# A hybrid SSD and retention block on one core: small products of several pieces placed at one step

## The chip, the cores and the metric

The kernel runs on one core of a Trainium2 chip. The metric is device time in microseconds (us), the median of the runs. The core has a matrix engine (TensorE, "PE" in the profile), VectorE ("DVE"), ScalarE ("ACT"), GpSimd ("POOL") and SyncE ("SP"), whose queue issues nearly all transfers here. Products are written to PSUM banks, and VectorE or ScalarE must read a bank before the next product may be written to it.

## What is computed

One decoder block over 1024 tokens of width 1024, in float32:

```python
h = rmsnorm(x, norm1_w)
z, xbc, dt, q, k, v, g = split(h @ w_in)          # width 5648
y_ssd = ssd_mixer(z, xbc, dt, ...)   # conv + SiLU, chunks of 128, 16 heads of 64, 2 groups
y_ret = retention_mixer(q, k, v, g)  # rotary q/k, chunks of 128, 8 heads of 128
x = x + concat(y_ssd, y_ret) @ w_out
h = rmsnorm(x, norm2_w)
x = x + (silu(h @ w_gate) * (h @ w_up)) @ w_down
out = rmsnorm(x, final_norm_w)
```

Within a chunk both mixers form scores, weight them with a decay matrix, multiply them with the values, add the product of the running state, and bring the state forward. These are products of 64 to 128 columns beside the wide projections.

## The kernel before, in words

The tokens are worked in two halves of 512 (four chunks of 128). Everything on TensorE is one list of *steps*: a step is one slice of 128 rows of a weight block times four tiles, each as three products of 512 columns (`three`), so 12 products. Steps 0 to 95 are the twelve input blocks of half 0, steps 96 to 191 those of half 1 (eight steps each), 192 to 223 the output projection of half 0, 224 to 255 that of half 1; the feed-forward part follows. `run_all` walks the list: for each step it loads and divides the weights of some later steps (`advance`), emits the 12 products, and then whatever was hung on that step with `at(step, function)`. A block's results are taken out of PSUM by `evac` at its last step, with high priority.

The mixers are such hung functions, laid over a stretch of steps by `spread`, which maps a list of (place, function) linearly onto it, the last place onto the last step:

- `ssd_pieces` (one round for each chunk and group, eight a half): `s0` loads the row of decays (E); `sz` loads the gate z; `s1` has a transpose and the B-C scores into one bank `bc` and four transposes of x into a bank `xp` and much VectorE and ScalarE work that makes the decay matrix E; `s2` has 16 products into a bank `yp` and one of 512 columns into a bank `sp`. VectorE then reads `yp` four times (line 685), multiplies by the gate (line 688), and adds `sp` to the state S (lines 700 and 701). `s3` has two one-column sums. A small float32 product appears as two instructions (two passes), a transpose as one. Half 0 lies on steps 64 to 93, half 1 on steps 152 to 185.
- `ret_pieces` (one round a chunk): `r1` loads v and g and has 8 score products; `r2` has 24 products (scores times values, the old state, the new state) and makes the normalised result `yn` on VectorE in a chain of some 40 instructions that ends at line 807; `r3` transposes `yn` in two lots of four (banks emptied by ScalarE at line 819) and stores it. Half 0 lies on steps 98 to 142, half 1 on steps 198 to 221.
- The q/k blocks rotate each of four token tiles (`rope`) and transpose them (`turn(t)`), one bank for each turn.

All small products take their banks from one tag, `M`, of three buffers; the input and output blocks use a tag `L` of five. Products keep their order in the program. The order of the instructions on VectorE and ScalarE is made when the program is built, from readiness and from priority (program order, moved forward for weight division and `evac`); on the chip each engine then runs its queue in that fixed order.

Of the kernel before, what the change touches and what calls it, by code (L numbers as in the profile page):

```python
# [65 lines left out]
def block_kernel(ctx: ExitStack, tc: tile.TileContext, x, norm1_w, w_in, conv_w, conv_b,  # L66
# [161 lines left out]
    def at(i, f):  # L228
        hooks.setdefault(i, []).append(f)
# [243 lines left out]
    def qk_block(h, b):  # L473

        d = H[h]
        c0, n = ((C_DT, 272), (C_Q + 256, 384), (C_K + 128, 384))[b]
        q0, nq, k0, nk = ((0, 4, 0, 0), (4, 4, 0, 2), (0, 0, 2, 6))[b]
        nh = nq + nk
        np_, p0 = nh // 2, (0, 2, 5)[b]

        def v(a):
            return a.rearrange("p (h j d) -> p h j d", j=2, d=32)

        def begin(blk):
            if b == 0:
                d["qk"] = T([P, 8, TH], "qk")
                d["ktok"] = T([P, NT, RH * RD], "ktok")
                d["dtr"] = T([P, NT, SH], "dtr", bufs=2)
            ev, rr = {}, {}

            def rope(t):
                def f():
                    g = h * NT + t
                    ab = T([P, 2, 512], f"m{14 + t % 2}")
                    A, B = ab[:, 0, :nh * RD], ab[:, 1, :nh * RD]
                    r = rr[t] = ev[t // 2][:, t % 2, :]

                    def bc(k):
                        return kc[:, k + 32 * g:k + 32 * g + 32].unsqueeze(1).unsqueeze(1) \
                            .to_broadcast([P, nh, 2, 32])  # L500
                    en = v(r[:, :nh * RD])
                    tt(v(A), en, bc(K_COS), op=ALU.mult)
                    tt(v(B), en, bc(K_SIN), op=ALU.mult)
                    ro = v(r[:, :nh * RD])
                    tt(ro[:, :, 0, :], v(A)[:, :, 0, :], v(B)[:, :, 1, :], op=ALU.subtract)
                    tt(ro[:, :, 1, :], v(B)[:, :, 0, :], v(A)[:, :, 1, :], op=ALU.add)
                    if nk:
                        nc.gpsimd.tensor_tensor(
                            d["ktok"][:, t, k0 * RD:(k0 + nk) * RD].rearrange(
                                "p (h d) -> p h d", d=RD),  # L510
                            r[:, nq * RD:nh * RD].rearrange("p (h d) -> p h d", d=RD),
                            kc[:, K_KD + k0:K_KD + k0 + nk].unsqueeze(2).to_broadcast([P, nk, RD]),
                            op=ALU.mult)
                return f

            def turn(t):
                def f():
                    m = bank("M")
                    for j in range(np_):
                        tr(m[:, j * P:(j + 1) * P], rr[t][:, j * P:(j + 1) * P])  # L520
                    act(d["qk"][:, p0:p0 + np_, t * P:(t + 1) * P],
                        m[:, :np_ * P].rearrange("p (j q) -> p j q", q=P), AF.Copy)
                return f

            def evac(t, pss):
                ps = pss[t]
                o = 16 if b == 0 else 0
                if b == 0:
                    stt(d["dtr"][:, t, :], ps[:, :SH], d["rt"](t), dtb, op0=ALU.mult, op1=ALU.add)
                if t % 2 == 0:  # L530
                    ev[t // 2] = T([P, 2, 512], f"x{6 + t // 2}")
                e = ev[t // 2][:, t % 2, :]
                if nq:
                    stt(e[:, :nq * RD].rearrange("p (h d) -> p h d", d=RD),
                        ps[:, o:o + nq * RD].rearrange("p (h d) -> p h d", d=RD), d["rt"](t),
                        kc[:, K_QD + q0:K_QD + q0 + nq].unsqueeze(2).to_broadcast([P, nq, RD]),
                        op0=ALU.mult, op1=ALU.mult)
                if nk:
                    act(e[:, nq * RD:nh * RD], ps[:, o + nq * RD:o + nh * RD], AF.Copy,
                        scale=d["rt"](t))  # L540
                at(blk.last + (1, 2, 4, 5)[t], rope(t))
                at(blk.last + (4, 5, 7, 7)[t], turn(t))
            return evac
        return Block(False, lambda: d["hT"], [(w_in, c0, n)], begin)

# [60 lines left out]
    def ssd_pieces(h, W):  # L606
# [3 lines left out]
        def s0(c, g):  # L610
            def f():
                r0 = c * SH + g * 8
                E = st["E", c, g] = W([P, 8, P])
                nc.sync.dma_start(E, rD[h][r0:r0 + 8, :].partition_broadcast(P))
            return f

        def sz(c, g):
            def f():

                if g == 0:  # L620
                    st[c] = T([P, 8, P], f"x{4 + c % 2}")
                nc.sync.dma_start(
                    st[c][:, 4 * g:4 * g + 4, :],
                    zD[h][g][:, :, c * P:(c + 1) * P].rearrange("j p q -> p j q"))
            return f

        def s1(c, g):
            def f():
                ex, xbc = d["ex"], d["xbc"]
                cs = slice(c * P, (c + 1) * P)  # L630
                r0 = c * SH + g * 8
                first = h == 0 and c == 0
                E = st.pop(("E", c, g))
                bT, cT = xbc[4][:, g, cs], xbc[5][:, g, cs]
                bc = bank("M")
                tr(bc[:, :P], bT)
                mm(bc[:, P:2 * P], bT, cT)
                b2 = T([P, 2, P], "bc", bufs=2)
                btok, cbm = b2[:, 0, :], b2[:, 1, :]
                act(btok, bc[:, :P], AF.Copy)  # L640
                tt(cbm, bc[:, P:2 * P], tri, op=ALU.mult)
                xp = bank("M")
                for j in range(4):
                    ch = 4 * g + j
                    tr(xp[:, j * P:(j + 1) * P], xbc[ch // 2][:, ch % 2, cs])
                xw = W([P, 2, 512])
                xdte, xdt = xw[:, 0, :], xw[:, 1, :]
                tt(v8(xdt), v8(xp), hbc(d["dt"], c, g), op=ALU.mult)
                for q in range(8):
                    hs = slice(q * SP_, (q + 1) * SP_)  # L650
                    act(xdte[:, hs], xp[:, hs], AF.Copy, scale=d["dte"][:, r0 + q:r0 + q + 1])  # L651
                C = None
                if not first:
                    C = W([P, 8, P])
                    act(C, E, AF.Exp)
                    tt(C, C, cT.unsqueeze(1).to_broadcast([P, 8, P]), op=ALU.mult)
                for q in range(8):
                    ts(E[:, q, :], E[:, q, :], ex[:, 0, r0 + q:r0 + q + 1], 0.0,
                       op0=ALU.subtract, op1=ALU.min)
                act(E, E, AF.Exp)  # L660
                tt(E, E, cbm.unsqueeze(1).to_broadcast([P, 8, P]), op=ALU.mult)
                st[c, g] = E, C, btok, xdte, xdt
            return f
# [43 lines left out]
        def s3(c):  # L707
            def f():

                if c == 0:  # L710
                    d["ss"] = T([P, SG, NT], "ss", bufs=2)
                b = bank("M")
                for g in range(SG):
                    mm(b[:, g:g + 1], st.pop(("q2", c, g)), ones[:, :1])
                act(d["ss"][:, :, c], b[:, :SG], AF.Copy)
            return f
# [4 lines left out]
        o = []  # L721
        for i, (c, g) in enumerate(seq):
            p = 0.5 * i
            o += [(p - 0.2, s0(c, g)), (p, s1(c, g)), (p + 0.25, sz(c, g)), (p + 0.8, s2(c, g))]
            if g == 1:
                o.append((p + 1.2, s3(c)))
        return sorted(o, key=lambda q: q[0])


    def ret_pieces(h, W):  # L730
# [80 lines left out]
        def r3(c):  # L811
            def f():
                yn = st.pop(c)
                o = W([P, 8, P])
                for b in range(2):
                    m = bank("M")
                    for j in range(4):
                        tr(m[:, j * P:(j + 1) * P], yn[:, 4 * b + j, :])
                    act(o[:, 4 * b:4 * b + 4, :], m.rearrange("p (j q) -> p j q", q=P), AF.Copy)
                nc.sync.dma_start(mixD[h][1][:, :, c * P:(c + 1) * P].rearrange("j p q -> p j q"),  # L820
                                  o)
            return f
        o = []
        for c in range(NT):
            o += [(c, r1(c)), (c + 0.5, r2(c)), (c + 1.6, r3(c))]
        return sorted(o, key=lambda q: q[0])


# [599 lines left out]
    s0 = I0["z0"].first  # L1428
# [30 lines left out]
    s0 = GU  # L1459
# [38 lines left out]
```

## Time and profile before

| | |
|---|---|
| median of 3 runs | 1456.47 us (1455.24 to 1456.62) |
| profiled execution | 1455.97 us, span 1454.2 us |
| TensorE products | 1437.1 us busy, 7278 instructions |
| VectorE | 1091.5 us busy |
| ScalarE | 670.7 us busy |
| granted TensorE clock | 0.998 mean |
| idle TensorE that the waits view lists | 5.5 us in 9 waits |

A row of a timeline is: start in us, duration, engine, line, operation, output<-inputs, and how many instructions were merged; a bracket at its end is the idle time before it and what ended it. Since products are pipelined, the time of a run of products is read from the start of its row to the start of the next row.

### The profile page before, as it was taken

The page shows a single profiled execution, that of the slowest core. Times are in us where ns is not written, and L with a number is a line of the kernel's source. Part 1 is how long each engine was busy: PE and PEld are TensorE (multiplying, and loading weights), DVE is VectorE, ACT ScalarE, POOL GpSimd, SP SyncE. Part 2 cuts the span into 40 slices and gives each one's busy share as a digit, 9 for nine tenths or more (in the row PEclk, how much of TensorE's full clock was granted, in tenths as well). Part 3 has the DMA queues.
Part 4 walks back from the last instruction along what each step waited for, and adds up shares of the span by engine and source line. Part 5 has one row for each costly group of instructions (what it writes and reads, how often), then busy time and mean ns, then how long its engine had stood idle before and what let it go on. Part 6 is the DMA issues. An engine that isn't in the chain of part 4 may idle for free.

```text
span 1454.2 us, 20840 instructions
## 1 busy us (share of the span) xinstructions
PE 1437.1 (99%) x7278; PEld 1195.5 (82%) x7278; DVE 1091.5 (75%) x2263; ACT 670.7 (46%) x1296; POOL 35.8 (2%) x66
## 2 busy tenths in 40 slices
PE   9999999999999999999999999999999999999996
PEld 7889878888889888888888878888888888888885
DVE  5677788767688898468764889987777778566767
ACT  6334467444354656324454643544444445422223
POOL 1002000000000000000000000000000000000000
PEclk9999999999999999999999999999999999999999
DMA  7333466474425458736543345644434446997863
GB/s 248 111 97 105 136 195 192 124 238 117 138 66 164 151 160 263 250 124 205 181 143 112 99 145 169 245 180 145 149 134 141 156 145 264 356 386 236 294 183 133
DMA packets 142313, 257.41 MB, mean 177 GB/s; under 512 B 11332, under 2 KB 71040, under 8 KB 142208
## 3 DMA queue, kind: packets, MB, share of 16 engines
q1 hardware_dynamic: 141072, 254.40, 53.5%
q8 instruction: 57, 0.93, 0.3%
q10 hardware_dynamic: 736, 1.12, 0.2%
q0 software_dynamic: 400, 0.57, 0.1%
q14 instruction: 48, 0.39, 0.1%
HBM read 185.46 MB, written 70.58 MB: 176 GB/s over the span
## 4 chain that ended last, share of the span: by engine, by line
PE 94%; DVE 3%; DMA 1%; ACT 1%; issue 0%; SPq 0%; DVEq 0%; ACTq 0%
PE L L179 70%; PE M L179 22%; PE M L182 2%; DMA zD<-x 0%; DMA m<-rD 0%; DVE x L1246 0%; DMA wr<-in_w_in_dram 0%; DVE x L1268 0%; DMA kc<-in_consts_dram 0%; DVE x L448 0%; ACT m L651 0%; DVE x L452 0%; DVE x L1282 0%; DVE wp L268 0%; DVE x L1292 0%
## 5 line engine op out<-in xcount | busy, mean ns | idle before, releaser
L268 DVE TENSOR_TENSOR wp<-wr,wp 128x512 fp32r<-128x512 f32 (+2 forms) x248 | 162.4, 655 | 140.6 <-ACT wp L267 135.4
L267 ACT ACTIVATE wp<-wr 128x512 fp32r<-128x512 f32 (+2 forms) x248 | 150.0, 605 | 253.9 <-PE L L179 206.6
L179 PE MATMUL L<-h,wp 128*128 128x512 f32 x1128 | 266.2, 392 | 0.0
L179 PE MATMUL L<-wp,h 128*128 128x512 f32 (+2 forms) x1248 | 259.9, 364 | 0.3 <-DVE x L448 0.3
L179 PEld LDWEIGHTS L<-h,wp 128*128 128x128 f32 x1128 | 209.9, 188 | 44.6 <-issue 1.0
L179 PEld LDWEIGHTS L<-wp,h 128*128 128x128 f32 x1248 | 215.2, 188 | 31.0 <-issue 5.3
L179 PE MATMUL L<-wp,m 128*128 128x512 f32 x768 | 180.2, 392 | 0.0
L179 PEld LDWEIGHTS L<-wp,m 128*128 128x128 f32 x768 | 142.7, 188 | 30.3 <-issue 0.5
L179 PE MATMUL L<-m,wp 128*128 128x512 f32 x360 | 86.5, 389 | 0.0
L179 PE MATMUL L<-m,h 128*128 128x512 f32 x321 | 79.8, 393 | 1.5 <-ACT h L1391 1.4
L179 PEld LDWEIGHTS L<-m,wp 128*128 128x128 f32 x360 | 67.6, 188 | 14.0
L179 PEld LDWEIGHTS L<-m,h 128*128 128x128 f32 x321 | 59.8, 188 | 15.8 <-ACT h L1391 2.6
L179 PE MATMUL L<-m,x 128*128 128x512 f32 x288 | 69.2, 389 | 0.0
L179 PEld LDWEIGHTS L<-m,x 128*128 128x128 f32 x288 | 54.1, 188 | 11.2
L179 PE MATMUL M<-m,x 128*128 128x512 f32 x240 | 57.7, 389 | 0.0
L411 DVE SCALAR_TENSOR_TENSOR m<-m,cols,m 128x512 f32<-128x512 f32 x72 | 52.2, 747 | 3.5 <-ACT m L409 3.2
L179 PEld LDWEIGHTS M<-m,x 128*128 128x128 f32 x240 | 45.1, 188 | 9.4
L179 PE MATMUL L<-h,m 128*128 128x512 f32 x207 | 51.3, 389 | 0.0
L179 PE MATMUL M<-m,m 128*64 128x128 f32 (+2 forms) x354 | 48.4, 299 | 0.0
L179 PEld LDWEIGHTS L<-h,m 128*128 128x128 f32 x207 | 38.9, 188 | 8.1
L179 PE MATMUL L<-h,x 128*128 128x512 f32 x180 | 43.5, 390 | 0.0
L179 PE MATMUL M<-m,wp 128*128 128x512 f32 x168 | 41.0, 391 | 0.0
(321 smaller groups left out, 2329.4 us busy)
## 6 DMA issues: line engine op xcount, KB each, us to landing
wr<-in_w_in_dram SPq DMA_DIRECT2D x144, 256.0 KB, 2.7
aD<-ktok SPq DMA_DIRECT2D x49, 512.0 KB, 3.2
m<-aD SPq DMA_DIRECT2D x47, 512.0 KB, 6.1
wr<-in_w_out_dram SPq DMA_DIRECT2D x64, 256.0 KB, 2.9
h<-aD SPq DMA_DIRECT2D x30, 512.0 KB, 5.2
aD<-x SPq DMA_DIRECT2D x28, 512.0 KB, 3.0
x<-in_w_gate_dram SPq DMA_DIRECT2D x22, 512.0 KB, 3.8
x<-in_w_up_dram SPq DMA_DIRECT2D x22, 512.0 KB, 3.8
```

Of the source, the lines that this page charges most:

```text
L179: tc.keep_in_program_order(nc.tensor.matmul(o, a, b, start=start, stop=stop, **kw))
L182: tc.keep_in_program_order(nc.tensor.transpose(o, a, ident))
L267: newest["act"] = act(pair[:, 0, :n], raw[:, :n], AF.Copy).ins
L268: newest["dve"] = tt(pair[:, 1, :n], raw[:, :n], pair[:, 0, :n].bitcast(F32), op=ALU.subtract).ins
L411: stt(dst, u[:, q:q + TH], w[q], dst, op0=ALU.mult, op1=ALU.add)
```

## The change

Three places of the hand-written order move. `turn(0)` of each q/k block goes one step later, to the step of `turn(1)`. In `ssd_pieces`, `s2` goes from 0.8 to 1.0 behind its round's start, which is the place of the `s1` two rounds later, and `s3` from 1.2 to 1.5, which is the place of an `s2` and an `s1` as well; as the list then ends 0.3 later and is laid over the same steps, all places move a little. In `ret_pieces`, `r3` goes from 1.6 to 1.5, the place of the next chunk's `r2`. Where two pieces have one place, the list keeps the order of the rounds: `s3`, `s2`, `s1`, and `r3` before `r2`. No operation is added or removed.

```diff
@@ -539,7 +539,7 @@
                 at(blk.last + (1, 2, 4, 5)[t], rope(t))
-                at(blk.last + (4, 5, 7, 7)[t], turn(t))
+                at(blk.last + (5, 5, 7, 7)[t], turn(t))
@@ -721,9 +721,9 @@
             p = 0.5 * i
-            o += [(p - 0.2, s0(c, g)), (p, s1(c, g)), (p + 0.25, sz(c, g)), (p + 0.8, s2(c, g))]
+            o += [(p - 0.2, s0(c, g)), (p, s1(c, g)), (p + 0.25, sz(c, g)), (p + 1.0, s2(c, g))]
             if g == 1:
-                o.append((p + 1.2, s3(c)))
+                o.append((p + 1.5, s3(c)))
@@ -822,7 +822,7 @@
         for c in range(NT):
-            o += [(c, r1(c)), (c + 0.5, r2(c)), (c + 1.6, r3(c))]
+            o += [(c, r1(c)), (c + 0.5, r2(c)), (c + 1.5, r3(c))]
```

## Rows read from the trace of the kernel before

**Rows 1.** The page, part 1: busy us of each engine.
```profile
PE 1437.1 (99%) x7278; PEld 1195.5 (82%) x7278; DVE 1091.5 (75%) x2263; ACT 670.7 (46%) x1296; POOL 35.8 (2%) x66
```
**Rows 2.** Timeline of TensorE around the turns of the first q/k block.
```profile
97.75 0.49 PE L182 MATMUL M<-kc,x 128*128 128x128 f32 x3
98.00 3.00 PE L179 MATMUL L<-h,wp 128*128 128x512 f32 x12
100.84 0.49 PE L182 MATMUL M<-kc,x 128*128 128x128 f32 x3
...
106.64 0.82 PE L182 MATMUL M<-kc,x 128*128 128x128 f32 x6
107.22 0.47 PE L179 MATMUL L<-h,wp 128*128 128x512 f32 x1
```
**Rows 3.** Timeline of TensorE: the end of an s2 (sp) with two turns behind it.
```profile
485.71 1.13 PE L179 MATMUL M<-m,bc 128*128 128x512 f32 x2
486.67 0.94 PE L182 MATMUL M<-kc,x 128*128 128x128 f32 x6
487.38 0.48 PE L179 MATMUL L<-wp,h 128*128 128x512 f32 x1
```
**Rows 4.** Timeline of VectorE behind the same s2: readers of yp and sp.
```profile
485.83 1.12 DVE L685 SCALAR_TENSOR_TENSOR u<-m,dcol,M 128x128 f32<-128x128 f32 x4 [0.40 <-PE M L179]
...
488.07 0.68 DVE L701 TENSOR_TENSOR S<-S,M 128x512 f32<-128x512 f32 x1
```
**Rows 5.** Timeline of TensorE: sp of the first and of the twelfth s2.
```profile
192.28 1.13 PE L179 MATMUL M<-m,bc 128*128 128x512 f32 x2 [0.24 <-DVE bc L641]
...
549.61 1.13 PE L179 MATMUL M<-m,bc 128*128 128x512 f32 x2 [0.77 <-ACT qk L521]
```
**Rows 6.** Timeline of VectorE: the four reads of yp of the same two.
```profile
195.56 1.11 DVE L685 SCALAR_TENSOR_TENSOR u<-m,dcol,M 128x128 f32<-128x128 f32 x4
...
549.95 1.12 DVE L685 SCALAR_TENSOR_TENSOR u<-m,dcol,M 128x128 f32<-128x128 f32 x4
```
**Rows 7.** Page, part 6: a weight load (KB each, median us to landing).
```profile
wr<-in_w_in_dram SPq DMA_DIRECT2D x144, 256.0 KB, 2.7
```
**Rows 8.** Timelines: the first r3 on TensorE; ScalarE's copies of first and eighth.
```profile
354.63 1.03 PE L182 MATMUL M<-kc,m 128*128 128x128 f32 x8
...
355.37 1.07 ACT L819 ACTIVATE m<-M 128x512 f32<-128x512 f32 x2
...
696.17 1.07 ACT L819 ACTIVATE h<-M 128x512 f32<-128x512 f32 x2
```
**Rows 9.** Timeline of TensorE, half 1: r2 of chunks 2 and 3, r3 of chunk 2.
```profile
667.26 0.60 PE L179 MATMUL M<-x,h 128*128 128x128 f32 x4
...
671.41 1.09 PE L179 MATMUL M<-x,ktok 128*64 128x128 f32 x16
...
688.44 0.60 PE L179 MATMUL M<-x,h 128*128 128x128 f32 x4
...
695.43 1.07 PE L182 MATMUL M<-kc,h 128*128 128x128 f32 x8
```
**Rows 10.** Timeline of VectorE, half 1: yn of chunk 1 ready; yn of chunk 2.
```profile
663.79 1.22 DVE L807 TENSOR_TENSOR h<-h,h 128x1024 f32<-128x1024 f32 x1
...
672.14 0.87 DVE L792 BATCH_NORM_STATS2 bs<-h 128x6 f32<-128x128 f32 x4 [2.24 <-ACT h L777]
...
688.29 2.72 DVE L860 SCALAR_TENSOR_TENSOR x<-L,rs,x 128x512 f32<-128x512 f32 x4
...
692.19 0.85 DVE L804 TENSOR_SCALAR h<-h,mv 128x128 f32<-128x128 f32 x3
...
694.08 1.20 DVE L807 TENSOR_TENSOR h<-h,h 128x1024 f32<-128x1024 f32 x1
```
**Rows 11.** Windows: stretch, its length, busy PE, PEld, DVE, ACT, POOL, PEclk, DMA.
```profile
190.00:220.00 30.00, 29.51 (x176) 22.55 (x175) 29.03 (x68) 17.00 (x44) 0.00 (x0) 1.00 0.59 175
...
836.00:838.00 2.00, 1.07 (x6) 0.82 (x7) 2.00 (x3) 1.29 (x3) 0.00 (x0) 1.00 0.05 6
```

## Prediction

> **What bounds the kernel now.** I read the engine shares first, then the timelines of TensorE and of whoever empties its banks. TensorE is busy 1437.1 us of a span of 1454.2 [rows 1]: its order of products is the path from start to end. So this change can act in two ways only: it changes the time that TensorE loses between small and wide products, and it adds or removes waits of TensorE. As TensorE has no slack, each wait is paid in full. VectorE, 75% over all, is at 29.03 of 30 us in the stretch where half 0's SSD work begins [rows 11]: there its queue runs late, and what TensorE wants from it comes late.
>
> **Where the pieces land.** I worked the places out by hand from `spread`'s formula. Between steps 16 and 223 the steps that carry small products fall from 80 to 56. Six `turn(0)` join `turn(1)`. Twelve `s2` now stand directly before an `s1` (before: on steps of their own or beside a turn or an `s3`): half 0 on steps 70, 73, 76, 79, 81, 84, half 1 on 159, 162, 165, 169, 172, 175. Six `r3` stand before the next chunk's `r2`: steps 112, 122, 132, and 205, 210, 215.
>
> **Fewer changes between small and wide products: a gain of 1.2 us.** Three transposes with 12 wide products take 3.09 us (97.75 to 100.84), three with 24 take 5.80 (100.84 to 106.64) [rows 2], so 12 wide products are 2.71 and three transposes alone 0.38. Of this 0.13 lies in the first wide products (98.00 to 100.84 is 2.84). Six in one go take 0.58 plus the same 0.13, 0.71 against 0.76. A merge saves 0.05 us; 24 merges, 1.2. The kinds with 64 rows aren't shown alone and merged side by side, so I let a merge be worth 0.02 to 0.08 us: 0.5 to 1.9.
>
> **s2 before s1: a loss of 4.5 us.** The three `M` banks go round. `s2` takes `yp` and `sp`, `s1` takes `bc` as third and `xp` as fourth, and the fourth is `yp`'s bank, which VectorE must have read four times. The kernel before has one such sequence: an `s2` with two turns behind it. Its six transposes take 0.71 us (486.67 to 487.38 [rows 3]) where six take 0.58 [rows 2]. The 0.13 is the wait for the reads, which end at 486.95 [rows 4], though VectorE stood ready and began at once. An `s1` has as much in front of the fourth bank as that turn, three instructions: a transpose and a product in two passes (`sp`, also one product, shows two [rows 3]). So 0.13 us each is the floor; twelve make 1.6. The ceiling takes VectorE's delays as they are now. `xp` would start 0.96 us (485.71 to 486.67) plus 0.33 after `sp`. At the first of the twelve that is 193.57, and the reads end at 196.67, 3.1 later; at the last 550.90 against 551.07, 0.2 [rows 5, 6]. The twelve sum to 13. I take 4.5, nearer the floor. The large delays came where VectorE had an `s1` from the step or two before, or the evacuation of z, in front of the reads. Now small groups come three steps apart as a rule, 8 us of wide products plus the group, and a round of `s1` and `s2` with three weight divisions is some 10 us of VectorE. It should have caught up at most of them, but not at all: two groups are only two steps apart, and half 1 has the rotations in between.
>
> **The turns behind step 172: 1.5 us.** There `s3`, `s2`, `s1`, `turn(0)` and `turn(1)` follow one another. `turn(0)` gets `sp`'s bank, whose reader, the sum into S, ends 3.04 us after `sp` starts (488.75 less 485.71 [rows 3, 4]). TensorE is there after 0.96 + 0.33 + 0.13 + 0.44 (four transposes) = 1.86. The wait is 1.2 at least; with VectorE a little behind I take 1.5, at most 2.5.
>
> **r3 before r2: 1.5 us.** `r3` uses two banks, `r2` the third and then again the first, in its second product. That comes after eight transposes and the two passes of the first product, ten instructions of 0.11 us, 1.09 us after `r3`'s start: at 355.72 for the first [rows 8]. ScalarE's first copy runs from 355.37 for half of 1.07 us, to 355.91. That is a wait of 0.19, and a little more until the product runs: 0.25, six times. The last copies began 0.74 after their transposes too [rows 8, 9]. Bounds: 0.15, and 0.50 where a weight copy is in front, so 0.9 to 3.0.
>
> **r3 of chunk 2 in half 1: 6.8 us, the largest term.** `r3` moves from step 216 to 215, before `r2` of chunk 3, so it is wanted at 688.44 instead of 695.43 [rows 9]. Its input `yn` is finished by VectorE at 695.28 (694.08 + 1.20) [rows 10]: now it is ready 0.15 us ahead. TensorE would stand from 688.44 to 695.28. VectorE's work in those 7 us doesn't hang on `r2` of chunk 3: it begins with the four evacuations of step 215 (2.72), then the last scalings (0.85 and one more), filled up with weight divisions and other work, then line 807 (1.20). If only the evacuations stay in front, 4.8 us remain; if everything else were ordered behind, 2.1. On the upper side, `r3` of chunk 1 is put before `r2` of chunk 2, so this chain, which begins at 672.14 after waiting for that `r2`, may begin up to 0.9 later in relation: 7.7. Chunk 1 escapes: ready at 665.01, wanted at 667.26 [rows 9, 10]. In half 0 the pieces are ten steps apart.
>
> **What costs nothing.** The loads of E and z and the stores of results move by a step with their pieces, all in SP's queue. The z load of chunk 2 in half 0 follows one step behind the store that frees its tile, where it was three. Weight loads stand behind it, with five weight buffers as cover; if that were gone, one load would be late by its 2.7 us [rows 7]. POOL's work isn't passed by anything. `rope` stays put. The 0.24 us that the first `sp` waits now [rows 5] should go, since it is a step further from the `s1` before it: 0.2 gained, up to 1.0 if the 0.77 us at the twelfth goes too, down to nothing.
>
> **The sum**, against the profiled execution of 1455.97 us (0.5 below the median of the runs): -1.2 - 0.2 + 4.5 + 1.5 + 1.5 + 6.8 = +12.9, so 1468.9; half a microsecond for the median makes 1469. With all bounds on one side the sum runs from -1.9 - 1.0 + 1.6 + 1.2 + 0.9 + 2.1 = +2.9 to -0.5 + 13 + 2.5 + 3.0 + 7.7 = +25.7: 1459 to 1482.
>
> **The rivals.** *yn comes in time.* VectorE's order is made anew when the program is built; if chunk 2's chain is ordered ahead of the fillers from 672.14 on, as it was for chunk 1, the 6.8 us vanish: 1463. For it: chunk 1's chain left 2.2 us of room. Against it: the high-priority evacuations stay in front.
>
> *The banks are free in time and the spacing clears the old waits.* `s2` now comes 5.6 steps behind its `s1` instead of 4.7. If VectorE then stands ready everywhere, `yp` is read while `sp` and `bc` run and `yn` is early as well, then only gains are left: the 24 merges, 0.24 and 0.77 us of waits [rows 5], some 2.2 to 2.9 us: 1453.5 to 1454.3. That is faster. It decides where the fourth bank's wait falls below 0.05 us, what a merge saves. Against it: 0.13 us is lost with VectorE ready [rows 3, 4].
>
> *Half and half.* `yn` comes in time and the bank waits are at their floors: -1.2 - 0.2 + 1.6 + 1.2 + 0.9 = +2.3, or 1459 at most, which counts as no change.
>
> *The clock.* The granted clock is 1.00 even where TensorE stood about half of two microseconds [rows 11]; no row shows a stall of near 7 us. If such a stall drops it to the 1.2 GHz level, each step run there costs up to 2.7 us more (12 wide products, [rows 2]): 1472 for one step. The Trainium skill, on the page TensorE: Matmul & The Clock Gate, section Why this matters for your kernels, warns of just that: an idle gap between bursts of matmuls brings the half clock back. No run here shows it.
>
> **How the numbers follow.** A measurement of this kernel tells 0.2% from no change, 2.9 us: faster is under 1453.6, slower over 1459.4. Forecast 0.52; `yn` in time 0.20; the clock 0.07; half and half 0.14; only gains 0.07. The first three are slower, less 0.02 for low ends: 0.77; no change 0.16; faster 0.07. The range from 1456 to 1479 leaves out the only-gains case, a part of half and half, and the top of the forecast's own range, together under 0.2.
>
> **What the profile of after would show.** Right: in the waits view a TensorE wait of 5 to 7 us on line 807 or its tile, near the 215th step; waits of 0.2 to 1 us on the transposes of `xp` released by line 685, and on `r2`'s second product released by line 819; about 24 fewer runs of small products. Wrong: `r3` of chunk 2 starts without a wait (the largest term falls), or the transposes of `xp` follow `bc` 0.11 us apart (the bank rule falls). A wait elsewhere that is longer than these would make the whole sum wrong.

## The result, and the profile after the change

The changed kernel takes 1481.7 us (median of 5 runs, 1481.0 to 1483.6) against 1456.5 before (5 runs, 1455.2 to 1458.2): 1.0173 times as long, with a 95% interval of 1.0161 to 1.0184. The direction was as forecast, the size was not: 1469 was the forecast and 1479 the end of the range.

| | before | after |
|---|---|---|
| profiled execution, us | 1455.97 | 1481.26 |
| its span, us | 1454.2 | 1479.5 |
| TensorE, busy us | 1437.1 | 1444.5 |
| granted TensorE clock, mean | 0.998 | 0.994 |
| idle TensorE that the waits view lists, us | 5.5 | 22.9 |

The page of after, the shares by engine (part 1); it answers [rows 1]:

```profile
PE 1444.5 (98%) x7278; PEld 1199.4 (81%) x7278; DVE 1092.2 (74%) x2263; ACT 672.5 (45%) x1296; POOL 39.2 (3%) x66
```

The same 7278 instructions keep TensorE 7.4 us longer, and VectorE does the same 2263 instructions in the same time. No engine has more to do; TensorE waits, and some of its products run slower. In the waits view of before no wait of TensorE is longer than 1.1 us. That of after (engine, tile, line, what ended the wait; us in all, how often, the longest):

```profile
PE M L182 <- DVE h L807: 7.2, 1, 7.2
PE M L182 <- DVE u L685: 5.0, 8, 1.6
PE M L182 <- DVE bc L641: 2.2, 1, 2.2
...
PE M L182 <- DVE S L701: 1.1, 1, 1.1
...
PE L L179 <- ACT x L468: 1.0, 1, 1.0
PE M L179 <- ACT m L819: 0.6, 1, 0.6
PE M L179 <- DVE q L692: 0.5, 1, 0.5
```

Of the lines left out here, 1391, 125 and 215 on its tile `m` wait in both kernels, and the rest are of 0.4 us or less. Nearly all that is new is on tile `M`, the three banks of the small products. Lines 807, 685, 701 and 819 were in the forecast; lines 641, 692 and 468 were not.

**Step by step.** The start of each step's first wide product, after less before, adds up where the time goes. The first wide product of all is 0.43 later already (6.22 us in before, 6.65 in after), where nothing was moved; by step 64 the difference is 0.23:

| at step | after later by, us | what lies between |
|---|---|---|
| 64 | 0.23 | input blocks of half 0, three merged turns |
| 87 | 3.86 | SSD of half 0: +3.6 |
| 134 | 5.38 | retention of half 0: +1.5 |
| 156 | 5.20 | |
| 186 | 13.96 | SSD and turns of half 1: +8.8 |
| 213 | 14.90 | `r3` of chunks 0 and 1: +0.9 |
| 217 | 24.20 | `r3` of chunk 2: +9.3 |
| 256 | 24.09 | |
| end | 25.28 | feed-forward part: +1.2 |

**The wait on yn.** Timeline of after around `r3` of chunk 2 in half 1 (start, duration, engine, line, operation, output<-inputs, count; in brackets the idle time before and what ended it); it answers [rows 9, 10]:

```profile
698.79 4.71 PE L179 MATMUL L<-wp,m 128*128 128x512 f32 x20
...
709.36 1.23 DVE L807 TENSOR_TENSOR h<-h,h 128x1024 f32<-128x1024 f32 x1
...
710.73 1.94 PE L182 MATMUL M<-kc,h 128*128 128x128 f32 x8 [7.24 <-DVE h L807]
...
717.60 1.65 PE L179 MATMUL L<-wp,m 128*128 128x512 f32 x6
```

TensorE has finished its wide products at 703.5 and gets `yn` at 710.6. What VectorE did in between is told by the chain of work that ended last, in that stretch (start, duration, what):

```profile
702.02 0.86 DVE h L804 x3
702.88 0.60 DVE wp L268
...
704.06 2.06 DVE x L860 x3
706.12 0.60 DVE wp L268
706.72 0.12 DVE m L842
...
707.30 0.59 DVE h L804 x2
707.89 0.66 DVE m L842
708.55 0.78 DVE h L804 x3
```

Four evacuations of step 215 (line 860, the first is among the lines left out), two weight divisions (268) and two divisions of prefetched inputs (842) stand between the first three of the eight scalings (804) and line 807. This is the order that the forecast described.

**The clock.** Windows of after: stretch, length, busy time of PE, PEld, DVE, ACT, POOL, then the granted clock, DMA share and GB/s.

```profile
484.00:486.00 2.00, 0.35 (x4) 0.35 (x4) 2.00 (x6) 1.44 (x2) 0.00 (x0) 1.00 0.12 43
486.00:488.00 2.00, 2.00 (x7) 1.62 (x6) 1.97 (x4) 1.70 (x8) 0.00 (x0) 0.50 0.38 102
...
704.00:708.00 4.00, 0.00 (x0) 0.00 (x0) 4.00 (x9) 1.31 (x3) 0.00 (x0) 0.98 0.48 139
708.00:712.00 4.00, 1.27 (x6) 1.30 (x7) 2.55 (x5) 0.15 (x1) 0.00 (x0) 0.50 0.18 58
...
716.00:718.00 2.00, 2.00 (x16) 1.48 (x15) 0.00 (x0) 0.30 (x1) 0.00 (x0) 1.00 0.00 0
```

Behind the stall on `yn`, and behind a shorter one at 484, TensorE runs at the 1.2 GHz level (0.50) for some us. That was a rival of mine, and its price stood outside the sum.

**A step that I had overlooked.** Timeline of after, step 156, TensorE and the one row of VectorE that the last product waits for:

```profile
482.22 0.28 PE L182 MATMUL M<-kc,m 128*128 128x128 f32 x1
482.33 0.39 PE L179 MATMUL M<-m,m 128*128 128x128 f32 x2
482.56 0.60 PE L182 MATMUL M<-kc,m 128*128 128x128 f32 x4
482.99 0.49 PE L182 MATMUL M<-kc,x 128*128 128x128 f32 x3
...
485.32 0.28 DVE L641 TENSOR_TENSOR bc<-M,kcB 128x128 f32<-128x128 f32 x1
...
485.65 0.61 PE L182 MATMUL M<-kc,x 128*128 128x128 f32 x3 [2.17 <-DVE bc L641]
```

An `s1` (banks `bc` and `xp`) is followed by `turn(0)` and now also by `turn(1)`: four banks in one run. The fourth is `bc`'s, which VectorE reads at line 641, at 485.32.

### The profile page after: what moved, and what is told of

Its sections match the earlier page's. It is cut to its first block, busy times and chain, and to the rows that moved or that the text cites. A ratio compares the mean times of both kernels' runs of the same rounds, so it can differ in the third digit from the quotient of the medians.

```text
span 1479.5 us, 20826 instructions
## 1 busy us (share of the span) xinstructions
PE 1444.5 (98%) x7278; PEld 1199.4 (81%) x7278; DVE 1092.2 (74%) x2263; ACT 672.5 (45%) x1296; POOL 39.2 (3%) x66
## 3 DMA queue, kind: packets, MB, share of 16 engines
q10 hardware_dynamic: 736, 1.12, 0.2%
## 4 chain that ended last, share of the span: by engine, by line
PE 84%; DVE 8%; DMA 3%; ACT 3%; issue 1%; SPq 0%; DVEq 0%; ACTq 0%
PE L L179 63%; PE M L179 19%; PE M L182 2%; DMA m<-mixD 1%; DVE wp L268 1%; DMA m<-rD 1%; DVE u L685 1%; DVE m L658 1%; ACT wp L267 1%; DMA x<-vD 0%; DVE x L1246 0%; DVE m L842 0%; DMA wr<-in_w_in_dram 0%; DVE x L215 0%; DVE m L661 0%
## 5 line engine op out<-in xcount | busy, mean ns | idle before, releaser
L179 PE MATMUL L<-wp,h 128*128 128x512 f32 (+2 forms) x1248 | 254.7, 361 | 1.0 <-ACT x L468 1.0
```

The costliest lines, as they stand in the source:

```text
L179: tc.keep_in_program_order(nc.tensor.matmul(o, a, b, start=start, stop=stop, **kw))
```

## The experiments

All ratios are to the kernel before, run on the same chip as the experiment.

**One part alone: turn_only, ssd_only, r3_only.** Each has one part of the three in the diff.

> Only the turns are moved (six turn(0) to the step of turn(1)); SSD and retention stay as before. Theory (fourth bank): six merges give back 0.3 us, but on step 156 s1 with bc and xp stands before two turns, so the second turn takes bc's bank and waits for VectorE, 2 us, and some slow products follow: 1460 us. Rival (the wait seen there in the changed kernel comes from the moved SSD pieces): no wait there, 1456.2 us.

> Only s2 and s3 are moved. Theory: each of the twelve s2 before an s1 waits 0.1 to 1.6 us for the reads of yp, half 0 loses 4 us and half 1 some 5: 1465 us, with TensorE waits put down to line 685. Rival (the loss of the changed kernel there is a change of VectorE's order and not of the banks): waits on other lines, or a loss under 3 us.

> Only r3 is moved. Theory: 1 us in half 0 and, in half 1, a wait of 7 us on line 807 with some 2 us of slow products behind it: 1467 us. Rival (yn of chunk 2 was late only because the other parts shifted VectorE's order): r3 waits under 2 us and the time is 1459 us.

| | time, us | ratio (95%) |
|---|---|---|
| turn_only | 1459.97 | 1.0021 (1.0011 to 1.0030) |
| ssd_only | 1467.41 | 1.0076 (1.0061 to 1.0091) |
| r3_only | 1469.13 | 1.0094 (1.0073 to 1.0114) |

All three bear the theory out; ssd_only and r3_only cost 2.4 and 2.1 us more than expected. By the medians the parts add up to 3.3 + 10.75 + 12.5 = 26.5, and the whole change costs 25.2: they are nearly independent. The waits views, in this order:

```profile
PE M L182 <- DVE bc L641: 1.9, 1, 1.9
PE M L182 <- DVE h L807: 1.5, 1, 1.5
```

```profile
PE M L182 <- DVE u L685: 5.8, 8, 1.7
PE L L179 <- ACT x L468: 2.2, 1, 2.2
```

```profile
PE M L182 <- DVE h L807: 7.2, 1, 7.2
```

Three readings. The turns, which I had put down as pure gain beside step 172, cost a wait on step 156 (line 641). They also leave `yn` 1.5 us late at the place that `r3` has *before* the change: that place had next to no room, and an edit that reorders VectorE a little can be felt there (0.4 us in before_M4 below, nothing in after_r3back). And line 468's wait is no bank of `M`: ScalarE empties a bank of the other tag, `L`, and its queue holds a prefetch's scaling (line 841) in front, which waits 1.12 us for its transfer from `mixD` in ssd_only.

**Was the fall of the clock the stall's doing? after_warm.** 32 products of ones, which nobody reads, stand before `r3` of chunk 2 in half 1 and fill the stall.

```diff
+                if (h, c) == (1, 2):
+                    b = bank("M")
+                    for _ in range(32):
+                        mm(b[:, :P], ones, ones)
```

> The changed kernel with 32 idle products of ones with ones, which nobody reads, in front of r3 of chunk 2 in half 1, so that TensorE works in the 7 us in which it waited. Theory (the products behind the wait are slow because TensorE's clock fell): granted clock 1.00 there, r2 of chunk 3 back from 6.9 to 5.3 us, 1480 us. Rival (r2 is slow because of waits of its own): r2 stays near 6.9 us and the time is 1481.7 us or more.

1481.06 us (1479.1 to 1482.4), 1.0170 times before: the median alone doesn't tell it from the changed kernel's 1481.7. The profile does. Windows of after_warm over the place of the stall and the group of `r3` and `r2`:

```profile
703.00:711.00 8.00, 7.86 (x70) 7.66 (x70) 7.31 (x14) 1.96 (x3) 0.00 (x0) 1.00 0.33 98
711.00:716.00 5.00, 4.97 (x39) 3.82 (x37) 0.00 (x0) 1.15 (x3) 0.00 (x0) 1.00 0.35 105
```

`yn` comes as late as before, but the clock stays at 1.00. From the start of `r3` to the next wide product it takes 5.35 us (710.49 to 715.84) where the changed kernel takes 6.87 (710.73 to 717.60). The fall of the clock behind this stall cost 1.5 us.

**Taking single steps back: after_r3back and after_turnback.**

```diff
-            o += [(c, r1(c)), (c + 0.5, r2(c)), (c + 1.5, r3(c))]
+            o += [(c, r1(c)), (c + 0.5, r2(c)), (c + (1.5, 1.6)[h], r3(c))]
```

> The changed kernel with r3 of half 1 alone back at 1.6. Theory: the 7.2 us on line 807, the slow products behind it and the two short waits on line 819 in that half go; as chunk 2 had no slack at the old place either, 0 to 1.5 us on line 807 may stay: 1472 us. Rival (the wait is made up elsewhere, as VectorE or the loads are late at the end of that stretch anyway): 1478 us or more.

1471.8 us (1.0107 times before): 9.9 us come back, line 807 is gone from the waits and the clock holds there. The edit also moves chunks 0 and 1, worth 0.9 by the table of steps, so about 9 us hang on the one place of chunk 2. In the profile the steps 213 to 217 lose 0.2 us instead of 9.3. The same profile loses 2.8 us more than the changed kernel up to step 186, 1.6 of it behind step 172, where the clock falls in this run and not in the other.

```diff
-                at(blk.last + (5, 5, 7, 7)[t], turn(t))
+                at(blk.last + (4 if (h, b) == (1, 1) and t == 0 else (5, 5, 7, 7)[t]), turn(t))
```

> The changed kernel with one turn of one block back at the old step: turn(0) of the second q/k block of half 1, which is on step 156 with an s1. Theory: the 2.2 us on line 641 and the slow products behind it, 1.6 us, go: 1478 us, granted clock 1.00 there. Rival (the clock falls there for another reason): the slow products stay and the time is 1480 us.

1478.45 us (1.0167 times before, interval 1.0139 to 1.0194): the times alone don't tell it from the changed kernel's 1.0173. The profile does: the wait on line 641 and the clock's fall behind it are gone, and at step 186 it is 10.2 us behind the kernel before, where the changed kernel is 14.0. Step 156 cost 3.7.

**A fourth bank: after_M4 and before_M4.** If the waits come from the ring of three, a ring of four must remove them. The kernel has eight banks in all, so tag `L` gives one up.

```diff
-... bufs={"L": 5, "M": 3}[tag])
+... bufs={"L": 4, "M": 4}[tag])
-            for t in "LLLLLMMM":
+            for t in "LLLLMMMM":
```

> The changed kernel with four M banks and four L banks in place of three and five. Theory (the fourth small-product bank is waited for): the waits on lines 685, 641, 701 and 819, some 9 us in the changed kernel, go, and with them the slow products behind step 156; the 7 us on line 807 stay: 1471 us if four L banks cost nothing. Rival (VectorE is late for any bank): the waits move to the fifth bank or to the L banks and the time stays over 1478 us.

> The kernel before with four M banks and four L banks. It prices the fourth L bank that was given up: theory (a block's first bank is emptied while its other three are finished) 1456 us, within 1.5; rival (each block's start waits for the evacuation before it) 24 blocks by 0.3 us or more, 1464 us.

after_M4 takes 1475.75 us (1.0139 times before), before_M4 1458.46 (1.0021). The waits view of after_M4:

```profile
PE M L182 <- DVE h L807: 7.4, 1, 7.4
PE M L182 <- DVE x L506: 4.3, 2, 4.1
...
PE M L182 <- DVE u L685: 1.1, 1, 1.1
```

The bank theory holds: lines 641, 701 and 819 are gone, 685 fell from 5.0 to 1.1, and `yn` is untouched. The time that I expected, 1471, was missed by 4.8 us. With `L` smaller and VectorE's order made anew, the rotation of a q/k tile (`rope`, line 506) ends 4.1 us after the turn wants it, and the clock falls there too. The kernel before pays 2 us for the smaller `L` without any of this.

**Keeping three banks and putting s1 in front: ssd_swap and swap_turns.** If all of the SSD's loss is that `yp` is overwritten, it must vanish when `s1` runs first. `s2` goes just behind `s1` (and the ring for `s1`'s results gets a ninth tile).

```diff
-... (p, s1(c, g)), (p + 0.25, sz(c, g)), (p + 0.8, s2(c, g))]
+... (p, s1(c, g)), (p + 0.25, sz(c, g)), (p + 1.001, s2(c, g))]
-                o.append((p + 1.2, s3(c)))
+                o.append((p + 1.5, s3(c)))
-    spread(ssd_pieces(0, ring(WS)), s0 + 8, I0["g1"].last - 2)
+    spread(ssd_pieces(0, ring(WS + ["wb0"])), s0 + 8, I0["g1"].last - 2)
```

(half 1 has the same ring; swap_turns merges five turns besides, leaving out the one on step 156).

> The kernel before with only the SSD pieces at the changed places, but s1 before s2 on their common step, so that yp and sp take the banks in place of bc and xp and a fourth bank is read long before it is wanted; the ring of decay tiles gets a ninth tile, which this order needs. Theory (the price is the bank that VectorE has yet to read, not the common step): waits on line 685 and 701 go, 1456 us, within 2. Rival (VectorE cannot follow when two pieces come at once): waits of 4 us or more on other lines, 1462 us.

> As ssd_swap, with five of the six turn(0) on the step of turn(1) too; the one on step 156 stays. Theory: 1455.5 us, at most 0.5 below ssd_swap. Rival: the turns meet an s1 or s2 on other steps and wait, 1458 us.

Both missed by far: 1474.16 us (1.0123, interval 1.0106 to 1.0140) and 1472.95 (1.0116). The waits view of ssd_swap, and its timeline at one group:

```profile
PE M L179 <- ACT m L651: 11.0, 7, 2.4
```

```profile
206.08 0.60 PE L182 MATMUL M<-kc,m 128*128 128x128 f32 x4
...
208.23 1.75 ACT L651 ACTIVATE wb<-M,dtw 128x64 f32<-128x64 f32 x8 [1.64 <-DVE wb L648]
210.03 1.12 PE L179 MATMUL M<-m,bc 128*128 128x512 f32 x2 [1.45 <-ACT wb L651]
...
211.19 0.28 ACT L640 ACTIVATE bc<-M 128x128 f32<-128x128 f32 x1 [0.27 <-PE M L179]
```

`bc`, `xp`, `yp`, `sp` are again four banks. The last, now `sp`, waits for the last reader of one that `s1` has just filled: eight ScalarE instructions that take 1.75 us together, themselves behind a VectorE instruction. `yp`'s four reads are the shorter wait. So my theory was too narrow: the loss isn't that of one order. In both orders the last of four banks waits for the readers of one that was filled just before.

I overlooked something that is the swap's own. `sp` takes `xp`'s bank and not `bc`'s, because the copy that reads `bc`'s bank (line 640) starts only behind `sp`: at nine groups within 0.06 us of its end. That copy goes to a tile `bc` in SBUF with two buffers, and with `s1` in front three rounds are open at once, so it waits until `sp` has read the oldest. The ring of decay tiles got its ninth tile; `bc` didn't get its third buffer. No run shows whether a swap with that third buffer waits as well.

**Moving yn forward: after_yn.** The normalisation of chunk 2 in half 1 gets a high priority down to line 807.

```diff
+                prio = tc.high_priority(PRIO if (h, c) == (1, 2) else 0)
+                prio.__enter__()
...
+                prio.__exit__(None, None, None)
```

> The changed kernel with high priority for the normalisation of chunk 2 in half 1, from its statistics to line 807. Theory (the 7 us are VectorE's order, other work is put between): the wait on line 807 falls under 2 us, the clock stays at 1.00 behind it, 1474 us. Rival (the chain itself is that long): the wait stays over 4 us, 1478 us or more.

1479.91 us (1.0157 times before): by the medians 1.8 us less than the changed kernel, where I expected 7 or more; the interval, 1.0140 to 1.0174, doesn't tell it from 1.0173. Timeline of after_yn (lines behind 790 have moved down by up to three: 809 is 807, 822 is 819, 844 is 841, 863 is 860):

```profile
700.72 1.21 DVE L809 TENSOR_TENSOR h<-h,h 128x1024 f32<-128x1024 f32 x1
...
704.45 0.66 PE L182 MATMUL M<-kc,h 128*128 128x128 f32 x4 [1.29 <-ACT h L822]
...
706.36 0.68 DVE L754 TENSOR_TENSOR h<-M,kcB 128x512 f32<-128x512 f32 x1
...
707.14 0.77 PE L179 MATMUL M<-x,h 128*128 128x128 f32 x2 [2.04 <-ACT m L844]
```

`yn` is ready at 701.9 and `r3` starts on time, so the cause of the 7.24 us was named rightly. But `r3`'s second lot waits 1.29 us for ScalarE's copy, and `r2` waits 2.04 us for its weighted scores. The view puts that down to line 844, but the scores (line 754) end at 707.04, 0.1 us before `r2` starts: VectorE makes them behind the four evacuations (863), two weight divisions (268) and a division of a prefetched input (845). The granted clock falls here as well: it is 0.50 in both windows from 710 to 718. The next waits took the first one's place, nearly whole.

**Only what finds free banks: turns_free.** The kernel before with the five other turn merges, and `r3` of half 1 at 1.8, still behind `r2`.

> The kernel before with only what found free banks: five merges of turn products (three in half 0, two in half 1; the one on step 156, whose last turn waits for line 641's read, is left out), and r3 of half 1 at p + 1.8, still behind r2. Theory: a merge saves about 0.05 us on TensorE and nothing waits, so 1456.0 to 1456.4, within 0.2% of the kernel before, and the waits view shows no VectorE entry above 0.5 us. Rival: any four products on one step cost a wait of 1.9 us and a fall of the clock, as on step 156: 1460 or more. Second rival: the merges are worth what products saved elsewhere suggest as a bound, 1 us: 1455.4.

1455.0 us against 1455.94, ratio 0.9994 (0.9985 to 1.0003): no difference that can be told. None of the change's new waits on VectorE shows, so the merges are harmless where the banks are free; whether each gains its 0.05 us can't be told in the time. No experiment gave a kernel that is measurably faster than the one before.

## Why the prediction was right in direction and too low

The sum said +12.9 for the profiled execution; it is +25.3. The last column is what was measured, term by term.

| step of the prediction | forecast, us | measured, us |
|---|---|---|
| fewer changes between small and wide | -1.2 | not seen singly; turns of half 0 as forecast |
| waits of `sp` in [rows 5] | -0.2 (-1.0 to 0) | -1.0 |
| `s2` before `s1` | +4.5 (1.6 to 13) | +7.05 |
| turns behind step 172 | +1.5 | +1.25 |
| `r3` before `r2` | +1.5 | about +2.8 |
| `r3` of chunk 2, half 1 | +6.8 | +7.2 |
| the clock | not in the sum | +3.1 |
| turns behind `s1` on step 156 | not seen | +2.2 |
| waits on lines 468 and 692 | not seen | +1.9 |
| behind step 256 | not seen | +1.2 |
| before the first wide product | not seen | +0.4 |

With the first term at -1.2 the last column makes 24.9, so about 0.4 us has no name. The two waits of `sp` in [rows 5], 0.24 and 0.77, are both gone. `r3` before `r2` is told by the pitch of the first products of `r2`: 0.80, 0.37 and 0.37 us too long in half 0, 0.38 and 0.59 for chunks 0 and 1 of half 1, and some 0.3 for chunk 2 as after_warm shows it. Lines 468 and 692 cost 1.33 and 0.61 by the steps that they stand on.

**Right: what bounds the kernel, and which waits come.** TensorE had no slack, and every wait was paid. `yn` was late by 7.24 us, against 6.8 from [rows 9, 10], with the four evacuations in front as described. The fourth bank is waited for where the prediction said, by the transposes of `xp` on line 685; so is `sp`'s bank behind step 172, by `turn(0)`, until line 701. The rival "`yn` comes in time" fell. The merges: three transposes' two runs of 0.49 in [rows 2] became one of 0.82, and from step 16 to 55 the three merged turns bring 0.14 us, 0.05 each as forecast.

**Mis-sized: s2 before s1.** A longer and the shortest of the twelve, timeline of TensorE in after:

```profile
194.92 1.12 PE L179 MATMUL M<-m,bc 128*128 128x512 f32 x2
...
196.59 0.63 PE L182 MATMUL M<-kc,m 128*128 128x128 f32 x4 [0.21 <-DVE u L685]
...
232.24 1.12 PE L179 MATMUL M<-m,bc 128*128 128x512 f32 x2
...
233.62 0.63 PE L182 MATMUL M<-kc,m 128*128 128x128 f32 x4
```

Without a wait `xp` starts 0.96 + 0.33 = 1.29 us after `sp`; here it is 1.67 and 1.38, waits of 0.38 and 0.09. The bracket shows only a part of it, because a product's end is modelled; so I take the pitch. The twelve are 0.38, 0.99, 0.66, 0.09, 1.80, 0.60 in half 0 and 0.10, 0.88, 0.64, 0.27, 0.36, 0.28 in half 1: 7.05 together. My value of 0.375 each lay between a floor and a ceiling that both came from rows; VectorE had caught up less often than I argued. The floor is there: in the two shortest VectorE began its reads 0.12 us after `sp`'s start, as in [rows 3, 4], and ended them 1.24 after it, and `xp` started 0.14 to 0.15 later, as in all twelve. It is 0.1 us and not 0.13.

**Failed: the clock left out of the sum.** The prediction gave it 0.07, because no row of before shows a stall of near 7 us, and priced it at 2.7 for one step as an alternative. But the forecast itself contained the stall. Whoever forecasts a stall longer than any in the trace must carry the clock as a bound of that term, not as an unlikely case: 6.8, up to 9.5. Measured: 1.5 us behind the stall on `yn` (after_warm), and about 1.6 on step 156, where the 3.7 that after_turnback gives back are a wait of 2.2 and the rest. That the rest is the clock is seen in the 24 wide products behind that place, in after and in after_turnback: 7.31 us where the clock is 0.50 and 0.65 in the windows from 486 to 490, and 5.74 where it holds.

```profile
485.96 7.31 PE L179 MATMUL L<-wp,h 128*128 128x512 f32 x24
```

```profile
483.64 5.74 PE L179 MATMUL L<-wp,h 128*128 128x512 f32 x24
```

With it counted at one step the forecast would have been 1472, still 10 too low. The Trainium skill (TensorE: Matmul & The Clock Gate, Why this matters for your kernels) warns that a gap between bursts of matmuls brings the half clock back; the trace agrees, with 0.50 after 7.24 us.

**Failed: step 156.** I looked for runs of four banks only where the diff put an `s2` in front. The rule "three banks" should have been laid over every step's list of pieces after the change, whatever their kind: `s1` and two turns also take four. It would have been found by counting banks on each of the 56 steps. On [rows 3]'s pattern I would have priced it at 0.13; in fact VectorE read the bank at 485.32, 2.3 us after ScalarE had begun its own read of it (483.01).

**Failed: the upper end.** All bounds on one side made 1482, and I cut the range at 1479 because I called the top of the sum unlikely. The bounds left out the two effects above, and both act upward only. That 1481.7 lies just under that 1482 is luck: the bounds had 13 us for `s2` before `s1`, where 7 were measured, and nothing for the clock and step 156.

**Still open.** Why the changed kernel loses another 1.2 us behind step 256, where nothing was moved: 0.4 of it is a wait on a weight division (line 215, tile `wp`) that the kernel before doesn't have, the rest are single wide products that start 0.1 us or so late. The evident guess is the remade order on VectorE and ScalarE; no run tested it. The 0.4 us without a name is open too.

## What to carry to other kernels

Before pieces are put on one step, count the buffers that each step's whole list takes, and for a run that takes one more than the ring has, price the last reader of its first buffers, queue included; swapping the pieces, as here, may only change the reader. A piece that uses a long chain's result has exactly the room that the trace shows between the chain's end and the use: here 0.15 us of room, and one step forward cost 9 us. If an edit stalls TensorE longer than anything in the trace does, add the price of a fallen clock to that term.

## What the runs showed of the hardware

The granted clock fell more easily than I had thought, and not by the length of the stall alone. It went to 0.50 (1.2 GHz) right after stalls of 1.87 us (turn_only), 2.17 and 7.24 us (after). It stayed at 1.00 after one of 2.19 us in ssd_only, with wide products before and behind it:

```profile
588.29 3.94 PE L179 MATMUL L<-wp,h 128*128 128x512 f32 x16 [2.19 <-ACT x L468]
```

```profile
588.00:590.00 2.00, 1.71 (x7) 1.42 (x8) 0.77 (x3) 2.00 (x5) 0.00 (x0) 1.00 1.12 370
```

ssd_swap has both in one run: 1.00 after a stall of 2.37 us at 536.3, and 0.50 after one of 1.94 at 551.7. Behind step 172 the same wait of 1.08 us on line 701 stands in after and in after_r3back. In after the clock stays at 1.00; in after_r3back, where 0.79 us of waiting on line 685 went ahead of it and 0.19 in after, it is 0.50 from 552 to 555, and the 24 wide products behind it take 7.34 us instead of 5.73 (first after, then after_r3back):

```profile
550.36 5.73 PE L179 MATMUL L<-wp,h 128*128 128x512 f32 x24
```

```profile
551.58 7.34 PE L179 MATMUL L<-wp,h 128*128 128x512 f32 x24
```

What decides between them no run here tells apart.
